# Steps of the mixers', norms' and splits' chains in a fused decoder layer: emitted by an estimate of engine and tile times instead of by counts

## The chip, the cores and the metric

One core of one Trainium2 chip runs the whole program. Its engines are PE (TensorE, matmuls), DVE (VectorE), ACT (ScalarE), POOL (GpSimd) and SP (SyncE, which issues most DMAs). Each engine runs its instructions in the order in which the program emitted them, and waits where an instruction's inputs are not ready; what is queued behind waits too. The metric is the device time of one execution in microseconds.

## The reference

One layer of a hybrid decoder, on 1024 prompt tokens and on 8 sequences of 4 new tokens with states of their own, all in float32:

```python
h = _rmsnorm(x, norm_mix)
p = jnp.einsum('btd,dp->btp', h, w_in) + b_in
...
out_a, buf, C, n, m = _mlstm_mixer(qk_a, v_a, o_a, i_a, f_a, conv_buf, C0, n0, m0, conv_w, conv_b, mlstm_norm)
out_b, S = _hgrn_mixer(q_b, f_b, i_b, g_b, S0, lb, hgrn_norm)
mix = jnp.concatenate([out_a, out_b], axis=-1).astype(x.dtype)
x = x + jnp.einsum('btm,md->btd', mix, w_out)
h2 = _rmsnorm(x, norm_ffn)
ff = jax.nn.silu(jnp.einsum('btd,df->btf', h2, w_gate)) * jnp.einsum('btd,df->btf', h2, w_up)
x = x + jnp.einsum('btf,fd->btd', ff, w_down)
```

The width is 1024. The mLSTM mixer (called A here) has 4 heads of 128: q and k go through a convolution over 4 tokens and a silu, two gates per head give weights by a running maximum, and a 128x128 state C is carried from chunk to chunk. The HGRN2 mixer (B) has 4 heads with a forget gate per channel and a state S. Each head's output is normalised and gated. A last norm follows the layer. Outputs are y and the new states of both sets of tokens.

## The kernel before

The 1056 tokens lie in the columns of three blocks b, of 288 (256 prompt columns and the 32 sample columns), 384 and 384. A matmul of float32 is done as three in a reduced format: a matrix is split into a high part (`whi` for weights, `HI` for activations) and a low part (`wlo`, `LO`), and `emit_k` adds hi·HI (L136), hi·LO (L138) and lo·HI (L139). A *unit* is one output tile of 128 rows for one block: 8 steps of k, 24 matmuls, called main matmuls here. A few units take their LO products last (L144).

Weight tiles arrive by DMA in `raw`; `split` (L94 to L99) copies the high part on ACT (L96) and subtracts it from the tile on POOL or DVE (L97). Rings of 5 hold `whi` and `wlo`. At the start, tiles of the three blocks' x come in with the first weights; `startup(b)` does the norm of blocks 1 and 2: squares (L1709 to L1716), a power on POOL (`nrs`, L1721), transposes that spread the result over columns (L1726, through `spread_nat`), the scaled X (L250), HI (L251) and LO (L247).

The units run in a fixed order: for each A head and block q, k, v, o, with a unit of gates inserted for each block of head 0; then for each B head and block f, q, v, g; then the output projection and the FFN. What a unit's result needs (bias, convolution, activation) is emitted right behind it by its `evac`; the first unit's convolution aside, `conv` runs through in one piece there.

Everything else that follows from the units is a *chain*, a Python generator: `gates(ps, b)` (softplus and scans of the gate rows, exps L356 to L358, transposes L368 to L370, copies into `cols` L371 and L372), `mix_a(h, b)` (masked weights W, transposes of k and v L551 to L558, the state's update U L574, `C` L584, the output O L595 to L597, squares L603, the norm's power L523, multiplies L608, transposes H L613), `mix_b(h, b)` (products of six levels through `prod` L800, factors `wib` L827, products of the two upper levels L883, transposes L897 and L900, U L914, O L934 and L936, squares L941, power L523, multiplies L946, H L951), the samples' chains, `startup` and `split`. `emit_k` calls `hook()` at every second k and at a unit's end. A generator yields a number: after so many hooks its next step is emitted. The numbers stand in tables (`GAW` for gates, `MAW` for `mix_a`, `SUW` for `startup`) or in the text (`yield 2`). So counts alone set how many main matmuls lie between two steps of a chain on PE, and what stands ahead of a step on the other engines. `finish(key)` runs hooks until a chain has ended.

Buffers come from rings too: PSUM tags mm (3 banks, units), mx (4 banks, chains, by `bank()`), so (1).

## Time and profile before

| | |
|---|---|
| median of 3 runs | 1381.51 us (1379.94 to 1382.96) |
| the profiled execution | 1379.56 us |
| its span in the profile | 1377.8 us |
| mean granted TensorE clock | 0.987 |
| busy: PE, DVE, ACT, POOL | 1325.5, 861.9, 554.7, 589.7 us |

The span runs from the first to the last recorded instruction. A row of a timeline gives the start in us, the duration, engine, line, operation, output <- inputs, shapes and how often it was repeated; brackets at its end give the idle time of the engine ahead of it and what released it. Rows of waits have the total, the number and the longest. In rows of windows, each engine's busy time is followed by its number of instructions, and PEclk is the granted clock as a share of full speed. The page's line of PE's busy tenths in 40 slices is 7 or 8 in the first three slices and 9 in all from the fourth to the 39th.

### The profile page before, as it was taken

Reading aid. Unit: us, or ns where it says so; the run is one execution under the profiler, and the core shown is the slowest. Engines: PE = TensorE matmul, PEld = TensorE weight load, DVE = VectorE, ACT = ScalarE, POOL = GpSimd, SP = SyncE. Lnnn points to the kernel's source line nnn. Section 1 sums busy time; section 2 is a strip of 40 time slices with the busy share of each in tenths; the row PEclk is TensorE's granted clock in tenths of the full one; section 3 lists DMA queues with packets and bytes.
Section 4 is the critical chain, followed back from the end, with each engine's and each line's share of the span. In section 5 each row is a group of like instructions: output and inputs, shape, how many; then the busy total and the mean of one; then the engine's idle time right before and its main releaser. Section 6 shows DMA issues by size and latency. Waiting matters only on the chain. (4 is left out here: it accounts for less than half of the span.)

```text
span 1377.8 us, 29359 instructions
## 1 busy us (share of the span) xinstructions
PE 1325.5 (96%) x11584; PEld 1295.9 (94%) x11584; DVE 861.9 (63%) x2048; ACT 554.7 (40%) x1307; POOL 589.7 (43%) x563
## 2 busy tenths in 40 slices
PE   7789999999999999999999999999999999999996
PEld 7679999899999998899999999999999999999995
DVE  7776657664555556644675667666765347777765
ACT  5654334234334334422435545544544342122232
POOL 4223213232222313122447666666666684444434
PEclk9999999999999999999999999999999999999997
DMA  9112112330111013543455657657664279878733
GB/s 339 39 43 80 59 48 75 100 99 19 48 39 43 32 50 118 160 155 134 165 178 192 230 196 259 205 218 253 212 218 169 79 259 354 301 272 296 273 151 126
DMA packets 111281, 216.44 MB, mean 157 GB/s; under 512 B 11248, under 2 KB 64136, under 8 KB 110632
## 3 DMA queue, kind: packets, MB, share of 16 engines
q1 hardware_dynamic: 110712, 214.31, 44.9%
q8 instruction: 91, 1.49, 0.4%
q10 hardware_dynamic: 432, 0.27, 0.1%
q14 instruction: 46, 0.38, 0.1%
HBM read 148.08 MB, written 66.45 MB: 156 GB/s over the span
## 5 line engine op out<-in xcount | busy, mean ns | idle before, releaser
L136 PE MATMUL mm<-HI,whi 128*128 128x384 f32 (+2 forms) x1160 | 378.0, 326 | 2.8 <-ACT HI L251 1.4
L139 PE MATMUL mm<-HI,wlo 128*128 128x384 f32 (+2 forms) x1160 | 362.3, 312 | 0.5 <-DVE wlo L97 0.5
L138 PE MATMUL mm<-LO,whi 128*128 128x384 f32 (+2 forms) x1136 | 353.0, 311 | 0.1
L136 PEld LDWEIGHTS mm<-HI,whi 128*128 128x128 f32 x1160 | 220.8, 190 | 7.4 <-issue 1.6
L139 PEld LDWEIGHTS mm<-HI,wlo 128*128 128x128 f32 x1160 | 220.4, 190 | 0.8 <-DVE wlo L97 0.7
L138 PEld LDWEIGHTS mm<-LO,whi 128*128 128x128 f32 x1136 | 215.3, 190 | 0.3 <-DVE LO L1018 0.3
L97 POOL TENSOR_TENSOR wlo<-raw,whi 128x512 fp32r<-128x512 f32 x86 | 113.5, 1329 | 211.9 <-ACT whi L96 167.2
L1222 POOL TENSOR_TENSOR wlo<-S,whi 128x512 fp32r<-128x512 f32 x78 | 110.7, 1425 | 90.7 <-ACT whi L1221 88.8
L1293 PE MATMUL mx<-T,whi 128*128 128x264 f32 x640 | 118.2, 284 | 0.0
L1293 PEld LDWEIGHTS mx<-T,whi 128*128 128x128 f32 x640 | 99.0, 188 | 0.0
L1346 POOL TENSOR_TENSOR LO<-rg,HI 128x528 fp32r<-128x528 f32 x52 | 70.3, 1362 | 63.3 <-ACT HI L1345 63.3
L1293 PE MATMUL mx<-HI,whi 128*128 128x264 f32 x320 | 91.0, 284 | 0.0
L1293 PE MATMUL mx<-T,wlo 128*128 128x264 f32 x320 | 90.9, 284 | 0.0
L1293 PE MATMUL mx<-HI,wlo 128*128 128x264 f32 x320 | 90.9, 284 | 0.0
L1293 PE MATMUL mx<-LO,whi 128*128 128x264 f32 x320 | 90.7, 283 | 0.0
L1434 DVE TENSOR_TENSOR fh<-fr,fh 128x512 fp32r<-128x512 f32 x80 | 67.6, 845 | 29.5 <-ACT fh L1429 29.2
L1520 DVE TENSOR_TENSOR X<-X,mx 128x264 f32<-128x264 f32 x160 | 65.7, 424 | 26.1 <-PE mx L1516 25.6
L1221 ACT ACTIVATE whi<-S 128x512 fp32r<-128x512 f32 x80 | 50.3, 630 | 68.1 <-DVE S L1210 64.6
L1345 ACT ACTIVATE HI<-rg 128x528 fp32r<-128x528 f32 x52 | 32.3, 641 | 103.0 <-PE mx L1516 30.2
L1293 PE MATMUL mm<-HI,whi 128*128 128x264 f32 x240 | 68.3, 284 | 1.3 <-ACT nt L1077 1.3
L1293 PE MATMUL mm<-HI,wlo 128*128 128x264 f32 x240 | 68.2, 284 | 0.0
L1293 PE MATMUL mm<-LO,whi 128*128 128x264 f32 x240 | 67.9, 283 | 0.0
(534 smaller groups left out, 3402.6 us busy)
## 6 DMA issues: line engine op xcount, KB each, us to landing
d_wf<-fh SPq DMA_DIRECT2D x60, 512.0 KB
rg<-d_ff SPq DMA_DIRECT2D x42, 528.0 KB
raw<-in_wA SPq DMA_DIRECT2D x31, 512.0 KB
whi<-d_wf SPq DMA_DIRECT2D x29, 512.0 KB
wlo<-d_wf SPq DMA_DIRECT2D x28, 512.0 KB
raw<-in_wgu SPq DMA_DIRECT2D x24, 512.0 KB
d_ff<-sg SPq DMA_DIRECT2D x40, 264.0 KB
rg<-in_wgu SPq DMA_DIRECT2D x20, 512.0 KB
```

The costliest lines, as they stand in the source:

```text
L97: (nc.gpsimd if pool else nc.vector).tensor_tensor(lo[:, s], raw[:, s], hi[:, s].bitcast(F32), op=OP.subtract)
L136: nc.tensor.matmul(ps[:, :n], wh, rh[:, k, :], start=(k == 0), stop=False)
L138: nc.tensor.matmul(ps[:, :n], wh, rl[:, k, :], start=False, stop=False)
L139: nc.tensor.matmul(ps[:, :n], wl, rh[:, k, :], start=False, stop=(k == nk - 1 and not late))
L1221: nc.scalar.activation(hi[:, s], t, AF.Copy)
L1222: (nc.vector if dve else nc.gpsimd).tensor_tensor(lo[:, s], t, hi[:, s].bitcast(F32), op=OP.subtract)
L1293: nc.tensor.matmul(ps[:, :QN], a[:, w], b_[:, kk, c], start=new and kk == 0 and x == 0, stop=kk == 3 and x == 2, skip_group_check=True)
L1345: nc.scalar.activation(h, src, AF.Copy)
L1346: (nc.vector if dve else nc.gpsimd).tensor_tensor(lw, src, h.bitcast(F32), op=OP.subtract)
L1434: nc.vector.tensor_tensor(lw, src, h.bitcast(F32), op=OP.subtract)
L1520: nc.vector.tensor_tensor(y, y, ps[:, :QN], op=OP.add)
```

## The change

The program now keeps an account of time while it is written. `estimate()` walks over each instruction that was emitted since the last call, gives it a duration by `cost`, lets it begin when its engine is free and its inputs are written (and its output's former buffer is read), and notes for each engine (`now`) and each piece of a tile (`wrote`, `read`) when it is done. A chain yields a condition `need(engine, tiles, banks=)` in place of a number: its next step is emitted at the first hook at which the tiles, and so many PSUM banks, are ready by the account. `hook` is called at every k, and does up to four steps of a chain.

```diff
+    def cost(e, op, x, n):
+        if e == "PE":
+            a = x.ins[0]
+            if a.dtype == F32R:
+                return 0.0076 + 0.000433 * n
...
+        if e == "DVE":
+            return 0.13 + (0.0018 if "Scan" in op else 0.00104) * n
+        if e == "ACT":
+            c = 0.1 + 0.00083 * n
...
+        return 0.25 + 0.002 * n
...
+    def need(e, *aps, banks=0, tags=(), lead=0.0):
+        def ok():
+            t = max([wrote.get(k, 0.0) for k in all_keys(aps)] + [0.0])
...
+            if e == "PE":
+                return t <= now["PE"] + lead
+            return t <= max(now["PE"], now[e]) + lead and now[e] <= now["PE"] + 2.0
+        return ok
...
+    def hook(part=False):
+        estimate()
         for e in list(active):
...
+            for _ in range(4):
+                if e not in active:
+                    break
+                if callable(e[2]):
+                    if not e[2]():
+                        break
+                elif part:
+                    break
...
-    NW, NRAW = 5, 2
+    NW, NRAW, NAUTO = 5, 2, 9
...
+        auto = t >= 2 and t < NAUTO
         for c in range(0, n, 512):
-            if c:
+            if auto:
+                yield need("ACT", raw)
+            elif c:
                 yield 2
...
-            if k % 2 and k < nk - 1 and not late:
-                hook()
+            if late:
+                hook(True)
+            if k < nk - 1 and not late:
+                hook(not k % 2)
...
-    GAW = ((1, 6, 14), (2, 3, 6), (2, 3, 6))
...
-        while b == 0 and ("cv", "k") not in done:
-            yield 1
-        while b and ("pS", 0, b - 1) not in done:
-            yield 1
+        yield need("ACT", f)
...
-        yield GAW[b][2]
+        yield need("PE", wi, wl, em, banks=2)
...
+        yield need("DVE", p0, p1_)
         nc.vector.tensor_copy(cols[:, c0:c0 + ncb, 0, :], p0[:, :ncb * 4].rearrange("p (c h) -> p c h", h=4))
...
-            acc = early(kind, h, b)
-            if acc is None:
-                acc = tl("c" + kind, 384, 1 if kind == "q" else 2)
+            acc = tl("qB" if kind == "q" else "ck")
...
-            if (h, b) == (0, 0):
-                start(conv(kind, h, b, raw, acc, rs), ("cv", kind), 1)
-            else:
-                for _ in conv(kind, h, b, raw, acc, rs):
-                    pass
+            start(conv(kind, h, b, raw, acc, rs), ("cv", kind, h, b), need("DVE", raw, acc))
...
-        yield w[2]
+        yield need("PE", kt, vt, banks=1)
...
-        yield w[4]
+        yield need("PE", W, C, qw, banks=1)
...
-        yield w[7]
+        yield need("PE", hn, banks=1)
...
+        for t in range(3):
+            x = xn[b, t]
+            yield need("ACT" if b == 2 else "DVE", *(x if isinstance(x, tuple) else (x,)))
+            rs = squares_nat(b, rs if t else None, (t,))
+        yield need("DVE", rs)
         rstd_nat(rs)
-        yield SUW[b][1]
...
+        yield need("PE", rs, banks=1)
+        pb = spread_nat(b, rs)
...
+            if m > 1:
+                e = nc.vector if now["DVE"] < now["POOL"] else nc.gpsimd
+                e.tensor_tensor(lv[:, m - 2, :], x[:, m - 2, :], hv[:, m - 2, :].bitcast(F32), op=OP.subtract)
...
-    start(startup(1), ("n1", 1), 5)
-    start(startup(2), ("n1", 2), 16)
+    start(startup(1), ("n1", 1), 1)
+    start(startup(2), ("n1", 2), 1)
...
-            start(split(nxt, True), ("w", nxt), {3: 7, 4: 10}.get(nxt, 1))
+            start(split(nxt, True), ("w", nxt), 1)
```

All other yields of `mix_a`, `mix_b`, the sample chains and the second parts of the evacuations are replaced in the same way. Since the order of chains is no longer fixed by counts, `finish` is called where a buffer would otherwise be taken too early, and some results get other buffers: q, k and the odd blocks' v, o lie in the rings qB, ck, cq and kB, `ngb` has two buffers, `sm` four, `nrs` five columns, and the last tile of x is loaded in three parts into kB, kB and cq. `load_bc`, which fetches a head's gate rows by DMA, is called behind k's unit and no longer behind q's. In `mix_b`, `step(16)` stands ahead of the copies into AT. The arithmetic is the same.

Three places show how instructions move. The first is POOL's queue near the program's start, from its first use for b=0's norm (the power that writes nrs) on. Before:

```order
L1721 TENSOR_TENSOR nrs<-nrs,mhalf 128x3
L247 TENSOR_TENSOR LO<-X,HI 128x288 x5
L97 TENSOR_TENSOR wlo<-wlo,whi 128x512 x2
L1721 TENSOR_TENSOR nrs<-nrs,mhalf 128x3
L97 TENSOR_TENSOR wlo<-whi 128x512 x2
L477 COPY sq<-st 128x32
L97 TENSOR_TENSOR wlo<-raw,whi 128x512 x2
```

After:

```order
L1895 TENSOR_TENSOR nrs<-nrs,mhalf 128x3
L365 TENSOR_TENSOR LO<-X,HI 128x288 x5
L213 TENSOR_TENSOR wlo<-wlo,whi 128x512 x2
L213 TENSOR_TENSOR wlo<-whi 128x512 x2
L213 TENSOR_TENSOR wlo<-raw,whi 128x512 x2
L1895 TENSOR_TENSOR nrs<-nrs,mhalf 128x3
L1921 TENSOR_TENSOR LO<-X,HI 128x384
```

The second power (b=1's norm) stood between the subtractions of tile 2 and those of tile 3 (wlo<-whi, a tile loaded into a whi buffer) and tile 4 (wlo<-raw,whi); now it stands behind all of them. On ACT, tile 4's copies, the first of them behind the first tanh before, stand ahead of every tanh.

The second place is DVE's queue around the copies into cols of gates(0), which TensorE's transposes write to mx. Before:

```order
L475 SCALAR_TENSOR_TENSOR st<-raw,st 128x384
L250 SCALAR_TENSOR_TENSOR X<-X,vec,mx 128x384
L460 COPY raw<-hist 128x3
L462 COPY hist<-raw 128x3
L470 SCALAR_TENSOR_TENSOR ck<-raw,vec,ck 128x384 x3
L475 SCALAR_TENSOR_TENSOR ck<-raw,ck 128x384
L250 SCALAR_TENSOR_TENSOR X<-X,vec,mx 128x384
L247 TENSOR_TENSOR LO<-X,HI 128x384
L250 SCALAR_TENSOR_TENSOR X<-X,vec,mx 128x384 x3
L371 COPY cols<-mx 128x2x4
L372 COPY cols<-mx 128x2x8
```

After:

```order
L583 SCALAR_TENSOR_TENSOR qB<-raw,vec,qB 128x256
L586 SCALAR_TENSOR_TENSOR qB<-rs,vec,qB 128x32
L487 COPY cols<-mx 128x2x4
L488 COPY cols<-mx 128x2x8
L1916 SCALAR_TENSOR_TENSOR X<-X,vec,mx 128x384 x4
L1921 TENSOR_TENSOR LO<-X,HI 128x384
```

Before, the copies stood behind the convolutions of b=1 and five of the eight scaled tiles X of b=2; now they stand behind the first convolution of b=0 and ahead of b=1's scaled tiles. In main matmuls ahead of them on PE: gates(0)'s transposes stand at 105 instead of 210, the spread of b=1 at 108 instead of 78, that of b=2 at 159 instead of 186, the transposes of the first `mix_a` at 228 instead of 216, gates(1) at 288 instead of 264, gates(2) at 393 instead of 354.

The third place is PE's queue in a chain of A in the steady part, head 1 and b=0: the step from the state's update U (vt, kt) to the output O (vt, W and C, qw), with main matmuls (mm) between. Before, U stands 18 main matmuls ahead of O; the end of this stretch:

```order
L136 MATMUL mm<-HI,whi 128x384
L138 MATMUL mm<-LO,whi 128x384
L139 MATMUL mm<-HI,wlo 128x384
L595 MATMUL mx<-vt,W 128x129 x2
L597 MATMUL mx<-C,qw 128x129
```

After, the whole of it:

```order
L710 MATMUL mx<-vt,kt 128x129 x2
L252 MATMUL mm<-HI,whi 128x384
L254 MATMUL mm<-LO,whi 128x384
L255 MATMUL mm<-HI,wlo 128x384
L252 MATMUL mm<-HI,whi 128x384
L254 MATMUL mm<-LO,whi 128x384
L255 MATMUL mm<-HI,wlo 128x384
L731 MATMUL mx<-vt,W 128x129 x2
L733 MATMUL mx<-C,qw 128x129
```

Six main matmuls lie between U and O where 18 lay (6 to 18 in the other steady chains of A). The same holds of the other steps of both mixers: from O to H in B, 54 main matmuls before (60 in one chain), 15 to 27 after (6 in one). From the output projection on, each engine's rows have the order of before, but for the numbers of buffers.

## The prediction

> **What bounds the kernel now.** I read the page first, for the share of each engine; then windows, to see in which stretch TensorE is idle or at a lower clock; then TensorE's waits; then the timelines of the engines behind the long waits.

> ```profile
> span 1377.8 us, 29359 instructions
> ...
> PE 1325.5 (96%) x11584; PEld 1295.9 (94%) x11584; DVE 861.9 (63%) x2048; ACT 554.7 (40%) x1307; POOL 589.7 (43%) x563
> ```

> TensorE is busy for 96% of the span, so at most 52 us of waiting (1377.8 − 1325.5) can go, plus what a low clock costs. The windows show where:

> ```profile
> core 0: us, PE busy (x) PEld busy (x) DVE busy (x) ACT busy (x) POOL busy (x), PEclk, DMA share, GB/s
> ...
> 24.00:56.00 32.00, 24.89 (x156) 23.29 (x154) 22.94 (x57) 19.57 (x40) 12.49 (x14) 1.00 0.42 148
> 56.00:70.00 14.00, 8.21 (x41) 8.00 (x40) 10.42 (x24) 8.87 (x17) 4.51 (x6) 0.76 0.00 0
> 70.00:102.00 32.00, 26.77 (x171) 25.73 (x169) 25.43 (x53) 15.71 (x31) 8.89 (x8) 1.00 0.15 47
> 102.00:111.00 9.00, 6.75 (x37) 6.65 (x38) 5.14 (x23) 5.70 (x19) 5.23 (x8) 0.62 0.38 105
> 111.00:130.00 19.00, 18.11 (x138) 17.68 (x137) 13.93 (x47) 8.41 (x25) 3.70 (x10) 1.00 0.16 46
> 130.00:575.00 445.00, 437.22 (x4583) 416.35 (x4583) 266.35 (x868) 175.94 (x518) 118.53 (x166) 1.00 0.22 68
> 575.00:1378.00 803.00, 784.27 (x6373) 779.63 (x6371) 501.30 (x948) 307.03 (x635) 427.64 (x340) 0.99 0.60 211
> ```

> From 24 to 130 us the idle time is 7.11 + 5.79 + 5.23 + 2.25 + 0.89 = **21.3 us**. The granted clock is 0.76 of 14 us and 0.62 of 9 us, which takes away 0.24 × 14 = 3.4 us and 0.38 × 9 = 3.4 us more, **6.8 us**. So the start holds 28.1 us that are no work. The mixers behind it (130 to 575 us) hold only 445 − 437.22 = **7.8 us**. The rest (575 us on: output projection and FFN) holds 18.7 us, but there the change leaves every engine's sequence as it was, but for a handful of rows and renumbered buffers: a term of 0. What is ahead of 24 us (b=0's norm and the first two tiles) also keeps its order, again 0.

> The start's waits have one pattern, work that is ready standing behind a step that is not:

> ```profile
> PE mx L555 <- DVE cols L371: 5.8, 1, 5.8
> PE mx L1726 <- POOL nrs L1721: 4.6, 2, 2.9
> PE mx L369 <- ACT gB L357: 4.4, 1, 4.4
> PE mx L883 <- DVE wib L827: 4.0, 5, 2.0
> ...
> PE mx L597 <- DVE C L582: 2.6, 2, 1.6
> PE mx L139 <- POOL wlo L97: 2.3, 2, 1.4
> PE mx L574 <- DVE kt L566: 2.3, 2, 1.8
> ...
> PE mx L136 <- ACT whi L96: 0.9, 1, 0.9
> ```

> **The change part by part.** *Weight tiles 3 and 4.* These rows of POOL and ACT are the cause of the waits on wlo and whi:

> ```profile
> 24.30 0.85 POOL L1721 TENSOR_TENSOR nrs<-nrs,mhalf 128x3 f32<-128x3 f32 x1 [4.89 <-DVE raw L460]
> 25.13 1.27 POOL L97 TENSOR_TENSOR wlo<-whi 128x512 fp32r<-128x512 f32 x1
> ...
> 28.51 1.28 ACT L474 ACT_TABLE_LOAD   x1 [4.43 <-DVE st L473]
> 29.81 0.44 ACT L474 ACTIVATE raw<-st 128x288 f32<-128x288 f32 x1
> 30.16 0.61 ACT L96 ACTIVATE whi<-raw 128x512 fp32r<-128x512 f32 x1
> ```

> POOL stood 4.89 us at the power for b=1's norm with tile 3's subtraction queued behind; ACT stood 4.43 us at a tanh with tile 4's copy behind it. After, both tiles' subtractions stand ahead of the power on POOL, and tile 4's copies ahead of every tanh on ACT. The three waits (2.3 + 0.9 = 3.2 us) go. Late next are b=1's HI tiles: its spread over PE, which stood behind 78 main matmuls, now stands behind 108, and ACT has the v copy, a 1024-wide square and the o activation among the HI copies. The next block of b=1 therefore waits; by hand I get about 2.4 us for it. This stretch gains little.

> *The columns of the gates, and the two long waits.*

> ```profile
> 61.95 1.66 DVE L250 SCALAR_TENSOR_TENSOR X<-X,vec,mx 128x384 f32<-128x384 f32 x3
> 63.53 0.16 DVE L371 COPY cols<-mx 128x8 f32<-128x8 f32 x1
> ...
> 63.74 0.48 PE L555 MATMUL mx<-ident,ck 128*128 128x128 f32 x1 [5.79 <-DVE cols L371]
> ...
> 103.97 0.26 PE L369 MATMUL mx<-ident,gB 4*128 4x4 f32 x1 [4.37 <-ACT gB L357]
> ```

> The copy into cols takes 0.16 us and stood behind b=2's scaled tiles (1.66 us for the last three); TensorE stood 5.79 us at the transposes behind it. After, gates(0) runs before any convolution, its transposes stand behind 105 main matmuls instead of 210, and the cols copies stand ahead of all of b=1's scaled tiles, while the transposes that wait for them stand behind 228 instead of 216. The 123 main matmuls between are 16 us of cover at 0.13 each. The wait of 5.79 us goes, and with it the slow clock that began in it. The price is on TensorE at place 105:

> ```profile
> 44.50 0.45 DVE L337 SCALAR_TENSOR_TENSOR AT<-AT,AT 4x288 f32<-4x288 f32 x1 [2.24 <-ACT AT L335]
> ...
> 47.84 0.41 DVE L354 TENSOR_TENSOR AT<-AT,C 4x256 f32<-4x256 f32 x1
> ```

> Between these two rows the gates' sums take 3.75 us on DVE. Six ACT steps of about 0.44 us (as the tanh at 29.81) and three table loads of 1.28 make 6.5 us more, 10.2 in all. The gates' unit ends at place 24, so 81 matmuls cover it, 10.5 us at 0.13 each (288 of 384 columns of 0.174 us, row below). With DVE's three wide squares of x ahead of the sums, I take 1.3 us of wait. The 4.37 us at 103.97 is gates(2), whose exps stood on ACT behind a tanh. It moves from place 354 to 393; gates(1) from 264 to 288. I take 1.1 us for gates(1), 0.2 for gates(2), and 0.6 for b=2's spread, which moves up from 186 to 159. The waits at L574 and L597 of the first two chains go: U moves from 240 to 248 and from 294 to 390.

> Sum of the start: 28.1 us before; after, 2.4 + 1.3 + 1.1 + 0.6 + 0.2 = 5.6 us, and no slow clock if no wait is long. **Gain 22.5 us.** The ends: 2 us left at best (each new wait fully covered), and 14 at worst: the rest of a wait like the 2.86 us that POOL's power caused at 49.83, three times over (8.6), and the 5.6. So the gain is 14 to 26.

> The number of table loads on ACT stays at ten and no arithmetic is added; new buffers cost no time. The moved DMA issues (broadcasts of the gates' rows now after k's unit, a third tile of x in three parts on SP's queue) wait for older readers of their buffers, and only the mixer's DVE steps wait for them, several units later. I cost them at 0; that cover lacking, each would be one wait of the size of a chain hop.

> *The mixers from 130 us on.* Counts gave each hop of a chain a fixed cover of main matmuls; now it has what the estimate asks for. The rows that price a hop:

> ```profile
> 160.11 0.33 PE L136 MATMUL mm<-HI,whi 128*128 128x384 f32 x1
> 160.29 0.33 PE L138 MATMUL mm<-LO,whi 128*128 128x384 f32 x1
> ...
> 435.48 0.39 PE L936 MATMUL mx<-C,qB 128*128 128x128 f32 x2
> ...
> 437.14 0.85 POOL L523 TENSOR_TENSOR sm<-sm,mhalf 128x3 f32<-128x3 f32 x1 [7.33 <-DVE AD L807]
> ...
> L946 DVE TENSOR_SCALAR kt<-mx,sm 128x128 f32<-128x128 f32 x29 | 8.4, 341 | 0.0
> L584 DVE SCALAR_TENSOR_TENSOR C<-C,wib,mx 128x129 f32<-128x129 f32 x21 | 7.3, 348 | 5.0 <-PE mx L574 4.5
> ```

> A main matmul of 384 columns starts 0.174 us after the one before. From the last O matmul of a B chain (435.48) to the end of the power (437.99) are 2.5 us, and three multiplies at 0.34, overlapped a little, make about 3.4 us until its transposes (H) can run; a block of two chunks needs about 2.7. Before, 54 main matmuls lay between O and H (60 once), over 7 us; after, 15 to 27, with what else stands there 2.6 to 5.0 us of TensorE's work, and 2.3 us in one chain, where O to H needs 3.4. The code prices the power at 0.25 + 0.002 × 3 = 0.26 us where the row has 0.85, so this hop comes up to 0.6 us early. From U to O of an A chain lay 18 main matmuls, now 6 to 18 in the steady part: 1.0 to 3.1 us, for two or three updates of C at 0.35 us and the last matmul's end, about 1.0 to 1.3. So nearly all of the spare cover is gone, but little of the need. Bounds for the 24 chains: 2 us, where only the one short hop waits, and 20, where each loses 0.8 us (the 0.6 of the power and some of a DVE queue that is 60% busy, 266 of 445 us). I take a third of a microsecond each, 8 us, nearer to the low end because what can be read off hop by hop is mostly at or above the need. Before it was 7.8, so the mixers' term is **+0.2**, between −6 and +12. The former large waits (L883 for wib, 4.0 us) should mostly go; small ones come at many chains.

> **Sum.** The profiled execution took 1379.56 us, of which 1377.8 are the span; it lies 2 us below the median of the runs, 1381.51, so that is the uncertainty of the base. 1379.56 − 22.5 + 0.2 = **1357**.

> **Rivals.** *A. The thin hops wait (1370 us).* The estimate takes DVE and POOL as independent. These rows say they are not:

> ```profile
> 90.64 6.05 POOL L97 TENSOR_TENSOR wlo<-raw,whi 128x512 fp32r<-128x512 f32 x4 [11.32 <-ACT whi L96]
> ...
> 95.70 1.40 DVE L350 TENSOR_TENSOR gA<-gA,gC 4x384 f32<-4x384 f32 x1
> 97.13 0.55 DVE L351 TENSOR_TENSOR gC<-gC,gm 4x384 f32<-4x384 f32 x1
> ...
> L97 POOL TENSOR_TENSOR wlo<-raw,whi 128x512 fp32r<-128x512 f32 x58 | 75.7, 1311 | 131.0 <-ACT whi L96 86.5 <-ACT sm L601 40.9 <-DVE lb L290 3.5
> ```

> The same sum on DVE took 1.40 us beside POOL's subtractions (until 96.7) and 0.55 after them; POOL's took 1.51 each there and 1.27 alone at 25.13. In the mixers these subtractions fill 75.7 us of 440, 17%. With some four DVE steps of two operands from SBUF in each chain, 96 in all, 16 meet one; at 0.85 us each that is 13 us that the thin hops cannot hide: 1357 + 13 = 1370. Against it: many such steps don't stand last in their hop, and the same meetings cost before hardly anything (7.8 us for all waits).

> [...]

> *B. A long wait stays at the start (1364 us).* The 2.86 us wait at 49.83 left the clock at 1.00 in its stretch; those of 5.79 and 4.37 us were followed by a slow one. If one new wait is as long as 4.4 us, where I count 1.3 to 2.4, it brings some 2.5 to 3 us and 3.4 of clock: 1364. For it: ACT holds three table loads and two wide squares in the same 15 us. Against it: no engine is full there (DVE 22.9, ACT 19.6 of 32 us from 24 to 56).

> *C. Slower (1385 us).* The place is POOL's queue in the mixers: after, a weight subtraction (1.31 us) can stand right ahead of a chain's power, because it is emitted when its own inputs are ready. If this happens to each of the 24 chains, with the 0.2 us that a power's own underestimate leaves, H waits 1.5 us each, 36 us: 1357 − 8 + 36 = 1385. It turns slower above (22.5 + 7.8) / 24 = 1.26 us per chain. Against it: of the 26 powers of the mixers 12 have a subtraction as the row ahead of them now, and 10 had before, when the cover was long; and the subtractions fill only 17% of POOL's time, so that most have ended.

> *D. Nothing gained (1379 us).* The start could be bound by arrivals, so that order cannot matter. Against it: the share of DMA is 0.42 from 24 to 56 and 0.00 from 56 to 70 us, where the longest wait is; and the long waits name cols and gB, which no DMA writes.

> **How the numbers follow.** Forecast (1350 to 1363) 0.52; below it, with the start's waits nearly all covered, 0.08; A and B together, 1363 to 1377, 0.28; D 0.05; C 0.07. A measurement of this kernel can tell about 0.2%, 2.8 us, from no change: faster 0.88, within 0.2% 0.05, slower 0.07. The range of 8 in 10 leaves out C, D and the ends of both sides: from 1347 (gain 26 at the start, 6 in the mixers) to 1373 (A in full and a part of B).

> **What would show it.** Right: from 24 to about 105 us TensorE's idle time is under 8 us and the granted clock 1.00; no row of waits for cols or gB above 2 us; wlo and whi of tiles 3 and 4 gone from the waits; the window of the mixers holds 5 to 12 us of idle time, in many pieces under 1 us, at transposes behind multiplies by the norm and at O behind C; from the output projection on the stretch is as long as before, within 2 us. Wrong: a stretch of lower clock in the start (B); waits of 1 us or more at most chains' H transposes (C), or DVE steps of twice their usual length ahead of TensorE's waits (A); a longer FFN, which would mean that buffers moved there have a price that I took as 0.

## The result, and the profile after

The changed kernel takes **1358.62 us** (median of 4 runs, 1357.0 to 1360.5), the kernel before 1382.24 us beside it (4 runs, 1379.94 to 1383.74). The ratio is 0.9831 with a 95% interval of 0.9809 to 0.9853. The prediction was 1357 us, 1347 to 1373, faster. The two profiled executions are 1379.56 us (span 1377.8) and 1360.21 us (span 1358.4): 19.4 us apart in span, where the medians are 23.6 apart, since the one of before lies below its median and the one of after above it.

The page of the changed kernel and its windows (columns as before; the mixers now end 20 us earlier, so that the last two windows are shifted):

```profile
span 1358.4 us, 29355 instructions
...
PE 1325.8 (98%) x11584; PEld 1295.0 (95%) x11584; DVE 860.1 (63%) x2051; ACT 558.0 (41%) x1309; POOL 594.1 (44%) x561
...
PEclk8999999999999999999989999999999999999997
```

```profile
24.00:56.00 32.00, 29.22 (x169) 27.20 (x168) 26.70 (x64) 23.40 (x50) 16.71 (x16) 0.95 0.44 147
56.00:70.00 14.00, 14.00 (x89) 13.67 (x87) 13.45 (x45) 7.72 (x21) 2.04 (x8) 1.00 0.01 1
70.00:102.00 32.00, 31.67 (x226) 31.35 (x227) 27.46 (x76) 21.48 (x46) 13.93 (x13) 1.00 0.31 100
102.00:111.00 9.00, 9.00 (x61) 8.96 (x60) 3.59 (x9) 2.56 (x6) 3.24 (x6) 1.00 0.17 60
111.00:130.00 19.00, 19.00 (x129) 18.93 (x128) 13.41 (x42) 7.36 (x24) 1.90 (x4) 1.00 0.07 25
130.00:555.00 425.00, 419.21 (x4461) 396.18 (x4460) 263.03 (x847) 172.34 (x503) 118.59 (x162) 0.99 0.23 71
555.00:1358.00 803.00, 784.84 (x6361) 780.75 (x6359) 496.18 (x940) 306.65 (x634) 428.32 (x340) 0.99 0.60 211
```

TensorE's busy time is the same (1325.5 and 1325.8 us). What went between these two executions is idle time: 52.3 us before, 32.6 after. The slow clock left most of the start but came back further on, so that in sum it cost the changed kernel's execution no less. By stretches: from 24 to 130 us 3.1 us of idle time are left of 21.3, a gain of **18.2**, and the slow clock costs 0.05 × 32 = 1.6 us in place of 6.8, a gain of **5**. In the mixers idle time is 5.8 in place of 7.8 us, a gain of 2, but a clock of 0.99 stands there now, some 3.4 us (two stretches, below). Behind the mixers idle time is 18.2 for 18.7 us, and a stretch of slow clock at 703 us costs 3.4 us more in this execution. Ahead of 24 us 0.5 us more are idle. The sum is −18.2 − 5 − 2 + 3.4 − 0.5 + 3.4 + 0.5 = −18.4, and the spans differ by −19.4. Of the last microsecond at most 1.0 lies at the program's end, where the clock is 0.50 for the last 13.6 us in place of the last 15.5.

TensorE's waits of the changed kernel, from 24 to 130 us and from 130 to 560:

```profile
PE mx L484 <- ACT AT L472: 1.7, 1, 1.7
PE mm L252 <- ACT HI L1918: 0.4, 2, 0.2
PE mx L255 <- POOL wlo L213: 0.3, 1, 0.3
...
PE mx L685 <- DVE ck L590: 2.0, 1, 2.0
PE so L842 <- DMA st<-in_S: 1.7, 1, 1.7
PE mx L864 <- DVE sjunk L861: 0.6, 1, 0.6
PE mx L1121 <- DVE kt L1116: 0.4, 1, 0.4
```

The waits for cols (5.8), gB (4.4), nrs (2.9) and wib (4.0) are gone. The largest that are new are the gates' transposes (L484, 1.7), k's convolution of one block (L685, 2.0) and a sample's state (L842, 1.7).

### The profile page after: what moved, and what is told of

Same layout as the page of the kernel before. It is cut to its first block, busy times and chain, and to the rows that moved or that the text cites. A ratio compares the mean times of both kernels' runs of the same rounds, so it can differ in the third digit from the quotient of the medians.

```text
span 1358.4 us, 29355 instructions
## 1 busy us (share of the span) xinstructions
PE 1325.8 (98%) x11584; PEld 1295.0 (95%) x11584; DVE 860.1 (63%) x2051; ACT 558.0 (41%) x1309; POOL 594.1 (44%) x561
## 5 line engine op out<-in xcount | busy, mean ns | idle before, releaser
L213 POOL TENSOR_TENSOR wlo<-raw,whi 128x512 fp32r<-128x512 f32 x86 | 116.8, 1368 | 201.4 <-ACT whi L212 201.3
```

The source lines that it names most:

```text
L213: (nc.gpsimd if pool else nc.vector).tensor_tensor(lo[:, s], raw[:, s], hi[:, s].bitcast(F32), op=OP.subtract)
```

## The experiments

Times are medians; each ratio is to the kernel before, timed beside it. The changed kernel is at 0.9831, so 0.01 of ratio is 13.8 us.

**e1, e3, e13 and e2. Is it the early tiles?** The first three edits are on the kernel before, by counts or by a wait taken out. e1 lets gates(0) run ahead of the convolution and holds the first `mix_a` where it was:

```diff
-        while b == 0 and ("cv", "k") not in done:
-            yield 1
...
         while ("gc", b) not in done or ("cv", "k") not in done:
             yield 1
+        if (h, b) == (0, 0):
+            yield 10
```

> The kernel before, with one part of the change alone: gates(0) no longer waits for k's convolution, so its transposes stand behind 150 main matmuls instead of 210 and the cols copies ahead of b=1's convolution; the first mix_a is held at 216, where it was. Theory (order at the start is the gain, and the cols copies are its largest piece): the 5.8 us wait for cols and the slow clock that began in it (3.4 us) go, at most 2 us of wait come at the transposes: 7 to 9 us faster than before, about 1373. Rival (the wait only moves to the next late tile, k's convolution or W): less than 3 us faster, with a wait of 3 us or more still at the first mix_a.

Measured: 1381.72 us, ratio 0.9996 (0.9986 to 1.0005). No gain: the rival held. The wait for cols is gone, but the first U waits 6.93 us for vt, and a main matmul 5.15 us for a wlo at 30.78 us.

e3 puts the subtractions of tiles 3 and 4 ahead of b=1's power:

```diff
-    SUW = {1: (2, 6), 2: (2, 13)}
+    SUW = {1: (6, 6), 2: (2, 13)}
...
-    start(startup(1), ("n1", 1), 5)
+    start(startup(1), ("n1", 1), 1)
...
-            start(split(nxt, True), ("w", nxt), {3: 7, 4: 10}.get(nxt, 1))
+            start(split(nxt, True), ("w", nxt), {3: 4, 4: 6}.get(nxt, 1))
```

> The kernel before, with other counts alone: the splits of tiles 3 and 4 begin earlier and b=1's power later, so that on POOL three of their four subtractions stand ahead of the power, and on ACT all of tile 4's copies ahead of the first tanh. Theory: the three waits for wlo and whi (3.2 us) go, but b=1's HI tiles are late next; 0 to 3 us faster, 1379 to 1382. Rival (these waits are independent of what follows): 3 us faster or more.

Measured: 1383.77 us, ratio 1.0010 (1.0000 to 1.0019). The three waits went, and the spread of b=1 waited 3.49 us for its power instead. The waits for cols and gB stayed (5.1 and 4.4 us).

e13 has both edits.

> The kernel before with both of these edits by counts. Theory: the pieces add, 8 to 12 us faster, about 1370 to 1374, that is 40 to 50% of the change's gain with no estimate at all. Rival (the gain needs the whole set of conditions, because each wait removed alone only moves): less than 5 us faster.

Measured: 1383.83 us, ratio 1.0012 (1.0000 to 1.0023). The rival held. TensorE's waits of e13 from 24 to 130 us, and the window:

```profile
PE mx L574 <- ACT vt L565: 9.7, 2, 7.1
PE mx L1726 <- POOL nrs L1721: 7.6, 1, 7.6
PE mx L367 <- ACT gB L355: 3.6, 1, 3.6
...
24.00:130.00 106.00, 84.88 (x518) 82.93 (x517) 77.46 (x197) 57.88 (x129) 33.10 (x43) 0.87 0.24 76
```

21.1 us are idle, as before (21.3), and the clock is lower. The waits for wlo, whi and cols have become waits of 7.6 us for the power and 7.1 us for vt, the next tiles in line.

The changed kernel has neither wait, and its rows show two different reasons. Here are POOL's power for b=1 and ACT's steps up to the first vt, in e13 and then in the changed kernel:

```profile
32.64 0.85 POOL L1721 TENSOR_TENSOR nrs<-nrs,mhalf 128x3 f32<-128x3 f32 x1 [1.88 <-DVE raw L458]
...
66.69 0.42 ACT L544 ACTIVATE W<-W 128x256 f32<-128x256 f32 x1 [1.21 <-DVE W L542]
...
68.11 0.52 ACT L331 ACTIVATE gB<-gA 4x384 f32<-4x384 f32 x1
...
70.49 0.52 ACT L333 ACTIVATE gB<-gB 4x384 f32<-4x384 f32 x1
...
71.47 0.36 ACT L565 ACTIVATE vt<-mx 128x256 f32<-128x256 f32 x1
```

```profile
31.98 0.85 POOL L1895 TENSOR_TENSOR nrs<-nrs,mhalf 128x3 f32<-128x3 f32 x1 [1.45 <-DVE raw L573]
...
50.45 0.53 ACT L448 ACTIVATE gB<-gA 4x384 f32<-4x384 f32 x1
...
52.84 0.52 ACT L450 ACTIVATE gB<-gB 4x384 f32<-4x384 f32 x1
...
59.23 0.42 ACT L680 ACTIVATE W<-W 128x256 f32<-128x256 f32 x1
59.55 0.37 ACT L701 ACTIVATE vt<-mx 128x256 f32<-128x256 f32 x1
```

The power ends at about the same time in both (33.49 and 32.83 us), but its spread stands behind 108 main matmuls in place of 78: the step comes later on TensorE. With vt it is the other way. The first U stands at 248 in place of 240, hardly later, and TensorE reaches it earlier, at 61.59 us; but vt is done at 59.92 in place of 71.83 us, because the exp of W ahead of it comes 7.5 us earlier on ACT and the steps of gates(1), with a table load among them (1.28 us each in the rows of both main kernels), no longer stand between the two. Here the tile comes earlier. The second U is of the first kind again: its kt is done at 86.59 us in the kernel before and at 85.54 in the changed one, while U moves from 294 main matmuls to 390.

e2 is the opposite, on the changed kernel: its gates(0) wait for k's convolution.

```diff
+        while b == 0 and ("cv", "k", 0, 0) not in done:
+            yield need("PE")
         yield need("ACT", f)
```

> The kernel after, with the gates of b=0 held until k's convolution is done, as before; its transposes then stand behind 234 main matmuls instead of 105. Theory: the early gates carry about a third of the start's gain, so 5 to 11 us are given back, 1364 to 1370, with a wait of several us at the gates' transposes or at the first mix_a, and a slow clock behind it. Rival (conditions adapt, so that everything behind moves by itself): within 3 us of the changed kernel, about 1359 to 1361.

Measured: 1370.83 us, ratio 0.9925 (0.9906 to 0.9945), 12 us given back, a little more than foreseen. From 24 to 130 us 13.4 us are idle. The conditions moved other steps along: the first `mix_a` begins behind 264 main matmuls in place of 228, the second behind 300 in place of 360. So early gates are worth nothing alone, and 12 us where the rest is in place and moves with them.

**e5. Is it the deferral?** By deferral is meant here that a step of a chain stands behind more main matmuls than before. In the changed kernel the second `mix_a` begins on TensorE behind 360 main matmuls, where 264 stood before; more buffers for q and v allow it. e5 takes that back with the wait that the kernel before had:

```diff
+            if (kind, h, b) == ("q", 0, 2):
+                finish(("pS", 0, 1))
             acc = tl("qB" if kind == "q" else "ck")
```

> The kernel after, with one finish added: b=2's first q waits, as before the change, until the second mix_a (head 0, b=1) has emitted its S and transposes. These then stand behind 264 main matmuls, as before, instead of 360; gates(0) stays early, at 105. New theory after the first four runs (the start's gain is the deferral of chain steps on TensorE, so that main matmuls fill the time in which DVE and ACT catch up; moving a tile earlier only moves the wait): 5 to 12 us are given back, 1364 to 1371, with a wait of 3 us or more at the second chain's U or kt/vt and a slow clock. Rival (the early gates are the gain by themselves): within 3 us of the changed kernel, 1356 to 1361.

Measured: 1368.33 us, ratio 0.9899 (0.9879 to 0.9919): 10 us given back. The windows and two rows of e5's timeline:

```profile
24.00:130.00 106.00, 97.86 (x606) 94.26 (x605) 85.44 (x222) 60.49 (x141) 36.75 (x44) 0.94 0.26 85
...
69.64 0.22 PE L484 MATMUL mx<-ident,gB 4*128 4x4 f32 x1 [2.71 <-ACT gB L472]
...
72.91 0.73 PE L753 MATMUL mx<-ident,kt 128*128 128x128 f32 x2 [2.03 <-DVE kt L748]
```

Idle time is 8.1 us in place of 3.1, and the clock 0.94 in place of 0.98 (0.04 × 106 = 4.2 us more). The mechanism is as expected, but not the places: the waits came at gates transposes (L484) and at H of the first chain (L753), and not at the second U. They show how much the edit moves: gates(1) went from 288 main matmuls to 264 and H of the first chain from 318 to 264, because the added `finish` lets the chains run on while no main matmul is emitted; the second U stands at 327, not at the 294 of the kernel before.

**e6, e7, e12. How thin are the hops in the mixers?** One number is changed, behind gates(2), so that the start stays:

```diff
             if e == "PE":
-                return t <= now["PE"] + lead
+                return t <= now["PE"] + (-0.8 if ("g", 2) in done else lead)
```

> The kernel after; behind gates(2), TensorE's steps of all chains are emitted only when their inputs have been ready for 0.8 us by the account. Theory (the hops' own waits are small; 5.8 us of idle time in the mixers, most of it at one wait for k's convolution and one for a DMA): within 3 us of the changed kernel, 1356 to 1361. Rival A of the prediction (thin hops wait at most chains): 4 us faster or more.

Measured: 1355.67 us, ratio 0.9805 (0.9790 to 0.9821), about 3 us below the changed kernel, at the edge of what the theory allowed; the intervals overlap. e7 has +0.6:

> The kernel after; behind gates(2), TensorE's steps of all chains are emitted up to 0.6 us before their inputs are ready by the account. Theory (hops have little spare cover left, so the account stands close to the edge): each of 24 chains waits at three to five hops for up to 0.6 us, 10 to 30 us slower than the changed kernel, 1368 to 1388. Rival (spare cover remains): within 4 us.

Measured: 1382.17 us, ratio 1.0000 (0.9990 to 1.0011): the whole gain is gone. e12 has −2.0:

> The kernel after; behind gates(2), TensorE's chain steps are emitted only when their inputs have been ready for 2.0 us by the account, about the cover that the counts gave. Theory (the change's gain is made at the start, and short hops in the mixers are no part of it): within 3 us of the kernel with 0.8 us, 1353 to 1358. Rival (short hops are part of the gain, since longer chains hold buffers longer and are then forced): 1360 or slower.

Measured: 1362.11 us, ratio 0.9853 (0.9839 to 0.9866), slower than with −0.8. The rival's number held; its reason, buffers that are held longer, was not shown. The mixers' windows of e6 and e7:

```profile
130.00:555.00 425.00, 419.51 (x4504) 398.31 (x4503) 273.12 (x858) 172.80 (x507) 118.81 (x163) 1.00 0.23 72
...
130.00:575.00 445.00, 426.92 (x4447) 393.94 (x4446) 267.73 (x842) 171.33 (x496) 117.74 (x162) 1.00 0.22 68
```

With +0.6 us 18.1 us are idle, in small waits at many steps. That is not the whole of it: of the 22.3 us between the two profiled spans (1380.7 and 1358.4), 14 are idle time and 8 are longer busy time of TensorE (1333.9 us for 1325.8) for the same matmuls, which was not followed up. TensorE's waits in the same stretch begin so:

```profile
PE mx L1083 <- DVE kt L1074: 2.8, 7, 1.1
PE so L842 <- DMA st<-in_C: 2.5, 3, 1.7
PE mx L685 <- DVE ck L590: 2.3, 2, 1.9
PE mx L1121 <- DVE kt L1116: 1.4, 4, 0.4
...
PE mx L961 <- POOL qw L990: 1.2, 5, 0.5
```

The changed kernel stands on an edge: 0.6 us the one way cost 23 us, while a cover of 0.8 us more costs nothing, and one of 2.0 costs 6 us against that. With −0.8 us the idle time in the mixers is 5.5 us, hardly less than 5.8: the 3 us of e6 are not idle time. In its profile the clock is 1.00 in the mixers, where the changed kernel's has two slow stretches; that this is the cause is argued from one profile of each.

**e8 and e11. DVE beside POOL.** The wait of 2.0 us for k's convolution has this ahead of it in the changed kernel's DVE timeline:

```profile
189.92 3.75 DVE L583 SCALAR_TENSOR_TENSOR qB<-raw,vec,qB 128x384 f32<-128x384 f32 x3
...
195.36 3.83 DVE L583 SCALAR_TENSOR_TENSOR ck<-raw,vec,ck 128x384 f32<-128x384 f32 x3 [0.33 <-ACT ck L561]
```

e8 takes the subtractions of tiles 9 to 19 off POOL, to DVE:

```diff
-            start(split(nxt, True), ("w", nxt), 1)
+            start(split(nxt, not 9 <= nxt < 20), ("w", nxt), 1)
```

> The kernel after, with the low part of weight tiles 9 to 19 subtracted on DVE instead of POOL, so that in A's phase no POOL subtraction of a weight tile runs beside a convolution on DVE. Theory (the 2.0 us wait for k's convolution at 198 us and the slow clock behind it come from convolution steps of 1.3 us beside POOL's subtractions, 0.62 alone): that wait and its 1.7 us of clock go, 2 to 4 us faster, about 1355 to 1357. Rival (DVE's added work, 22 subtractions of some 0.7 us, comes late instead): the same or slower, with other waits for DVE.

Measured: 1356.87 us, ratio 0.9815 (0.9799 to 0.9830). The same rows in e8:

```profile
188.44 1.93 DVE L583 SCALAR_TENSOR_TENSOR qB<-raw,vec,qB 128x384 f32<-128x384 f32 x3
190.29 0.68 DVE L213 TENSOR_TENSOR wlo<-raw,whi 128x512 fp32r<-128x512 f32 x1
...
192.96 1.93 DVE L583 SCALAR_TENSOR_TENSOR ck<-raw,vec,ck 128x384 f32<-128x384 f32 x3
```

The convolution's three steps take 1.93 us again and the wait is gone, so its cause is shown. Other waits came, at V's transposes (2.2 us behind kt, 1.7 behind a sample's state) and for states from memory (2.8), and 7.2 us are idle in the mixers: of the 2 to 4 us that were expected, 1.8 appear, within the uncertainty. e11 leaves each step on its engine and tells the account of this meeting: behind gates(2) a DVE instruction with two inputs from SBUF (`two`) waits in the account until POOL's instruction has ended.

```diff
...
+                if two or e == "POOL":
+                    if e == "DVE": t = max(t, now["lk" + e])
+                    now["lkPOOL" if e == "DVE" else "lkDVE"] = t + cost(e, op, x, n)
...
```

> The kernel after; behind gates(2) the account lets a DVE instruction with two operands from SBUF wait until a POOL instruction under way has ended. Theory (convolutions beside POOL's subtractions are what the account misses): the wait for k's convolution falls from 2.0 to below 1 us; 1 to 4 us faster than the changed kernel, 1355 to 1358. Rival (one wait in 425 us is too little to matter, and other steps move): 1357 to 1361.

Measured: 1363.77 us, ratio 0.9863 (0.9840 to 0.9886). Both expectations failed, the theory's most: 10.3 us are idle in the mixers, at V's transposes behind kt (1.6 us), H (1.4), U (1.4) and samples' states (2.9). That the DVE instruction waits for the whole of POOL's is the author's assumption; the rows show longer steps, 3.75 us for three in place of 1.93. Putting the meeting into the account did not give a better order here; why these steps came out worse was not followed up.

**e9 and e10. A filler in the FFN's wait, and the best version.** The profiles of before, after, e1 to e3, e5 to e8 and e13, ten in all, have a wait of 3.2 or 3.3 us at the FFN's first products; in four of them, the changed kernel's among them (a clock of 0.50 from 703.1 to 709.9 us), it is followed by a stretch at half rate, in the others, as in that of before, it is not. e9 fills it:

```diff
+            if (u, p, j) == (0, "P5", 0):
+                dum = bank("so")
+                for _ in range(22):
+                    nc.tensor.matmul(dum[:, :QN], wh[:, 0:128], rh[:, 0, c], start=True, stop=True)
```

> The kernel after, with 22 matmuls of 264 columns that nobody reads (2.7 us) put on TensorE into its 3.2 us wait at the start of the FFN products, at 701 us; nothing else moves. Theory (a window of 3.41 us that is idle for more than about half of its time is followed by one or two at half rate; the windows run on a fixed grid, so that this wait is hit in some executions only): no slow clock near 703 us; the median falls by 1 to 3.4 us against the changed kernel, 1355 to 1358, and the executions lie closer together. Rival (the wait has nothing to do with the two levels of the executions): the same 1358.6 or slower.

Measured: 1359.85 us, ratio 0.9831 (0.9812 to 0.9851). The slow stretch is not in its profile, and 0.6 us of the wait are left; the median did not move. The range of the times stayed as it was (1357.8 to 1360.9), so the two levels of the changed kernel's runs (1357.0 twice, and 1360.2 and 1360.5) are not explained by that stretch. The rival held.

e10 has that filler, the lead of e6 and another price for a DMA in the account:

```diff
-                end = now["dma"] + 1.8
+                end = now["dma"] + (3.0 if ("g", 2) in done else 1.8)
```

> The version that the runs point to: the kernel after with that filler, a lead of -0.8 us for TensorE's chain steps behind gates(2), and 3.0 us instead of 1.8 for a DMA's fixed time in the account behind gates(2). Theory: no slow clock at 703, the wait for the sample states (1.7 us and its slow clock) gone or shorter than 1 us, 3 to 6 us faster than the changed kernel, 1352 to 1356. Rival (each wait that is removed comes back at the next hop): 1357 to 1360.

e10 measured 1355.21 us, ratio 0.9798 (0.9779 to 0.9816): the fastest of all, with e6 (0.9805) beside it. Two kernels with the lead of −0.8 agree, 3 us below the changed one; filler and DMA price add nothing that can be told. The sample's state no longer waits in e10, and other hops wait in its place (1.7 at the convolution, 1.4 at a sample's U).

## Why the prediction was right, and where it was wrong

**The start: right in size, half right in its cause.** Forecast was a gain of 22.5 us, from 28.1 to 5.6; measured are 18.2 of idle time and 5 of clock, 23 us. But the prediction booked each wait on the tile that was late ("The wait of 5.79 us goes, and with it the slow clock that began in it"), and let it go because the tile came earlier. e1, e3 and e13 make these tiles early and gain nothing: the time comes back at the next late tile. Waits booked one by one could be summed because the change also deals with the tiles that are late next, and of how it does so the prediction had one half. Some tiles come earlier, as it said, vt by some 12 us against e13. Other steps come later on TensorE, and main matmuls run in the meantime, which it passed over in half a sentence ("U moves from 240 to 248 and from 294 to 390"), and which the first U hardly does. e5 takes part of the second half back and loses 10 of 24 us; e2 takes the early gates back and loses 12. Since each of them also moves steps of the other half, their shares are not separated, and no run adds later steps alone to the kernel before. That the sum came out to within 1 us is in part luck: what the late waits cost was booked too high (5.6 us, 3.1 measured), and the slow clock that was to be gone cost 1.6.

**Tiles 3 and 4: right.** The three waits went (0.3 us left), "this stretch gains little" held in e3, and what was late next there was not b=1's HI but the power ahead of it. In the changed kernel, where the spread stands at 108, HI waits 0.4 us, not 2.4.

**The gates' transposes: right to half a microsecond.** 1.3 us were taken, 1.7 and 0.2 came. The price that was missed is the clock: this wait was followed by 3.4 us at half rate, 1.7 us lost, and "no slow clock if no wait is long" fell. gates(1), gates(2) and b=2's spread were priced at 1.9 us together and cost 0.3.

**The mixers: nearly right as a sum, wrong in form.** The forecast was 8 us of small waits for 7.8; there are 5.8, of which 3.7 are two waits, and few small ones. A third of a microsecond at each chain was too much: the need read off the rows is met by the order. e7 shows that it is just met, e6 and e12 that 0.8 us of cover is enough and 2.0 too much. With the clock (+3.4) the stretch cost 1.4 us against the 0.2 forecast.

**The FFN: right** in idle time (18.2 for 18.7 us); the slow stretch there was not in the sum.

**The rivals.** A (thin hops beside POOL) names a true effect: in e8, without POOL's subtractions, three convolution steps took 1.93 us in place of 3.75. Convolution steps of 128x384 took 0.62 us alone (34 in the changed kernel, 44 before). Where a POOL tensor operation overlapped them by more than 0.1 us, they took 1.36 us on average in the changed kernel (11 took 1.52 to 1.62, three 0.62) and 1.07 before (two 1.53, two 0.62), while scaling by a tile in PSUM (X) took at most 0.61 either way. By what mechanism is not shown. But it was one wait of 2 us and not 13 us. B expected a wait of 4.4 us for a slow clock; waits of 1.7 to 2.0 were enough. C and D did not occur.

## What to carry to other kernels

In a stretch where several engines lag behind the bound one, a wait is not a property of the tile it names: three times, making that tile early only moved the wait to the next late one. So a forecast that takes a wait away should ask which tile is late next, and for each one whether it comes earlier itself or other work of the bound engine now stands ahead of the step that waits. Buffers that let a dependent step be late are one way to the second. An order made by an estimate should get some slack: here 0.6 us too little cost the whole gain of 23 us, and 0.8 us more cost nothing.

## What the runs showed of the hardware that was not expected

```profile
194.50:197.90 3.40, 3.40 (x21) 3.40 (x21) 3.00 (x6) 1.87 (x4) 1.98 (x2) 1.00 0.71 255
197.90:201.30 3.40, 1.43 (x11) 1.11 (x10) 2.75 (x6) 1.59 (x4) 1.30 (x2) 1.00 0.39 131
201.30:204.70 3.40, 3.40 (x15) 3.40 (x14) 1.37 (x3) 1.45 (x3) 2.46 (x3) 0.51 0.07 28
204.70:208.10 3.40, 3.40 (x28) 3.40 (x26) 1.57 (x5) 0.58 (x1) 0.34 (x1) 0.99 0.08 23
```

The wait of 1.97 us lies in one window, and the next has 0.51 of the clock and 15 matmuls where 21 and 28 stand in full ones; 1.7 us are lost. The FFN's wait of 3.3 us in the kernel before shows the other case:

```profile
717.20:720.60 3.40, 2.13 (x18) 1.92 (x17) 1.99 (x4) 1.80 (x4) 0.00 (x0) 1.00 0.01 4
720.60:724.00 3.40, 1.53 (x12) 1.31 (x11) 2.23 (x3) 1.95 (x5) 3.04 (x3) 1.00 0.12 40
724.00:727.40 3.40, 1.93 (x13) 1.73 (x14) 0.65 (x2) 2.58 (x7) 3.40 (x3) 1.00 0.00 0
```

It is longer, but the grid cuts it in two, 1.87 and 1.47 us (the 1.27 us in the window ahead are another wait), and the clock stays at 1.00. All 14 profiles of this study, from 24 to 1300 us, windows at full rate, by their time without a matmul:

```
us without a matmul   windows   followed by half rate
under 1.0                5059       0
1.0 to 1.5                 39       2
1.5 to 1.7                 25       2
1.7 to 1.9                 15       9
1.9 and more               31      31
```

So in these profiles the limit lies near 1.7 to 1.9 us without a matmul in one window, about half of it, though 4 of the 64 windows with 1.0 to 1.7 us were followed by half rate too, which these counts do not explain. What a wait cost in clock depended on where it fell: 1.7 us for the 1.97 us above, nothing for the 3.3 us that the grid cut in two. In the changed kernel the FFN's wait has 2.44 us without a matmul in the window from 699.7 us, and the two windows behind it, from 703.1 us on, have a clock of 0.50.
